# The merge of attention branches: its elementwise work from GpSimd to VectorE, its PSUM banks from the scores' pool

## The chip, the cores and the metric

One core of one Trainium2 chip runs the whole program. The metric is the time of one execution on the device in microseconds; the kernel before has a median of 3433.43 us over three runs (3427.34 to 3434.07).

## The reference, cut to what matters

One step of a hybrid decoder layer over a prompt of 2048 tokens and a sample group of 8 x 8 tokens. Half of the layer's mixing width is dilated sliding-window attention (8 heads of 64), the other half an RWKV-7 recurrence. Then come the output projection and an MLP. In the attention every head evaluates three key sets ("branches" b = 0, 1, 2 with window and dilation (128,1), (512,4), (2048,16)) and merges their outputs by their softmax denominators:

```python
mall = max(maxs[0], maxs[1], maxs[2])
for mx, dn, o in zip(maxs, dens, outs):
    sc = jnp.exp(mx - mall)
    num = num + sc[..., None] * o
    den = den + sc * dn
out = num / den[..., None]
```

## The kernel before

The kernel runs in stages: input projection and recurrence, the attention of the prompt (from about 1218 to 1760 us of the span), the output projection with the sample's attention, the MLP. The change is in the attention of the prompt. The order of the instructions on each engine isn't written out by hand: the Tile framework lays it out ahead of time, by the order of the program as priority and with a planner's own costs for when each operand is there. On the chip each engine then runs its queue in order, and waits on semaphores. A pool's tiles are given out in the order of the program; a tile asked for while all of its pool's buffers are taken waits for a release.

Four calls of `attention(p, ...)` (L1056), one for each pair of heads, each run three branches of four groups; a group is two steps (branches 0 and 1) or one (branch 2), so a call has twenty steps. A step makes score tiles on TensorE (PE) in the PSUM pool "sc" (L1087, L1088, three banks), adds the bias and takes the row minimum on VectorE (DVE, L1090), takes exponentials on ScalarE (ACT), transposes (L1105, pool "pt", two banks), copies back by ACT or DVE in turn, and multiplies with the values into "o" (L1112, two banks). After each group ACT copies o to `ob[b]` (L1116 to L1120). The tile ob[0] has two buffers, ob[1] and ob[2] one each.

`merge(p, ob, st)` (L1127) is a generator; its steps run during the next call, two for each `pump()` (L1390) at the end of an attention step. It spreads row statistics over groups (`zst` L1135, `mv2` L1136, on GpSimd, POOL), brings them into a common layout by small products (L1144, L1149, L1155), copies these to `sw` by ACT, takes minimum, exponentials, denominators and weights on DVE and ACT, sends the weights through DRAM (wD, wrow, L1190 and L1193), and then, for four groups of columns and three branches, spreads them over partitions by a product (L1200), multiplies ob[b] by them on DVE (L1201) and adds up the branches (L1203). The merge of call 3 runs after the attention.

The same `pump()` also advances `recurrent_half()` (L1232) by one step, by two at every eighth: the recurrent rows' part of the output projection. It loads weights and inputs by DMA on SP's queue, splits them in two parts on POOL (L1239, L1240, tiles fm and fw), makes 64 groups of twelve products (L1263) in the PSUM pool "ax", which has one bank, adds the residual on DVE (L1265, tile fr) and stores to rD (L1266). The merges of calls 0 to 2 take their PSUM tiles from "ax" too; that of call 3 takes them from "sc".

After the prompt's attention, `sample_attention` (L1279) loads cached keys and values, with its own PSUM pools "sp" and "ax" in the banks that the attention has left, and the products of the output projection (L1541) run beside it; the last columns of the projection need the sample's result.

Of the kernel before, what the change touches and what calls it, by code (L numbers as in the profile page):

```python
# [9 lines left out]
F32 = mybir.dt.float32  # L10
F32R = mybir.dt.float32r
AF = mybir.ActivationFunctionType
ALU = mybir.AluOpType
# [4 lines left out]
P = 128  # L18
# [12 lines left out]
def bc(ap, axis, n):  # L31
    a = ap.unsqueeze(axis)
    shape = list(a.shape)
    shape[axis] = n
    return a.broadcast_to(shape)
# [136 lines left out]
def _build(ctx, tc, nc, I, O, dbg, upto):  # L172
    V, S, PE, G = nc.vector, nc.scalar, nc.tensor, nc.gpsimd
# [4 lines left out]
    def tsc(out, in0, s1, s2, op0, op1):  # L178
        V.tensor_scalar(out, in0, s1, s2, op0, op1)

    def tt(out, a, b, op):
        V.tensor_tensor(out, a, b, op)  # L182

    def act(out, in_, func, bias=0.0, scale=1.0, **kw):
        S.activation(out, in_, func, bias=bias, scale=scale, **kw)  # L185

    def pool(**kw):
        if kw.get("space") is not DRAM:
            kw["reuse_waits"] = "tile"
        return tc.tile_pool(**kw)  # L190
# [798 lines left out]
    psc = ph2.enter_context(pool(name="psc", bufs=3, space=PSUM, side="right"))  # L989
    ppt = ph2.enter_context(pool(name="ppt", bufs=2, space=PSUM))  # L990
    pax = ph2.enter_context(pool(name="pax", bufs=1, space=PSUM))
# [64 lines left out]
    def attention(p, pump, ahead):  # L1056
# [66 lines left out]
        if p < 3:  # L1123
            ahead["bias", p + 1, 2] = bias_load(p + 1, 2)
        return merge(p, ob, st)

    def merge(p, ob, st):  # L1127


        def mp():  # L1130
            return psc.tile([P, 512], F32, name="sc") if p == 3 else pax.tile([P, 512], F32, name="ax")

        for ty in range(2):
            for x in range(2):
                G.tensor_tensor(zst[:, x, :, :, 4 * ty:4 * ty + 4], bc(st[:, x, 1, :, ty, :].rearrange("p g q -> p q g"), 3, 4), bc(bc(mk1, 1, 4), 1, 4), ALU.mult)  # L1135
                G.tensor_tensor(mv2[:, ty, x], bc(st[:, x, 2, :, ty, :], 3, 8), bc(bc(rr2, 1, 4), 1, 4), ALU.mult)  # L1136
            yield
        sw = at.tile([P, 6, P], F32, name="sw")
        ps = mp()
        flat = st.rearrange("p x b g t c -> p (x b g t c)")  # L1140
        for x in range(2):
            for g in range(4):
                c0 = x * 96 + g * 8
                PE.matmul(ps[32 * g:32 * g + 32, x * P:x * P + P], flat[:, c0:c0 + 32], ident, start=True, stop=True, tile_position=(0, 32 * g))  # L1144
        for x in range(2):
            for q in range(4):
                for g in range(4):
                    c0 = 256 + x * P + q * 32
                    PE.matmul(ps[32 * g:32 * g + 32, c0:c0 + 32], zst[:, x, q, g], rr1, start=True, stop=True, tile_position=(0, 32 * g))  # L1149
        act(sw[:, 0:4].rearrange("p a n -> p (a n)"), ps, AF.Copy)  # L1150
        yield
        ps = mp()
        for g in range(4):
            for ty in range(2):
                PE.matmul(ps[32 * g:32 * g + 32, 0:256], d2[:, g, ty], mv2[:, ty].rearrange("p x g c m -> p (x g c m)"), start=(ty == 0), stop=(ty == 1), tile_position=(0, 32 * g))  # L1155
        act(sw[:, 4:6].rearrange("p a n -> p (a n)"), ps[:, 0:256], AF.Copy)
        yield

        def nat(x, b):
            v = sw[:, 2 * b + x]  # L1160
            return v if b == 0 else v.rearrange("c (q n) -> c n q", q=(0, 4, 16)[b])

        def alike(ap, b):
            return ap if b == 0 else ap.rearrange("c (n q) -> c n q", q=(0, 4, 16)[b])

        nall = at.tile([P, P], F32, name="nall")
        V.tensor_copy(nall, nat(0, 0))
        for b in (1, 2):
            tt(alike(nall, b), alike(nall, b), nat(0, b), ALU.min)
        sc = at.tile([P, 3, P], F32, name="scw")  # L1170
        for b in range(3):
            tt(alike(sc[:, b], b), alike(nall, b), nat(0, b), ALU.subtract)
        act(sc, sc, AF.Exp)
        yield
        dn = at.tile([P, P], F32, name="dn", tag="nall2")
        dm = at.tile([P, P], F32, name="dm", tag="nall")
        tt(dn, sc[:, 0], nat(1, 0), ALU.mult)
        for b in (1, 2):
            tt(alike(dm, b), alike(sc[:, b], b), nat(1, b), ALU.mult)
            tt(dn, dn, dm, ALU.add)  # L1180
        tsc(dn, dn, 1e-30, None, ALU.max, ALU.bypass)
        V.reciprocal(dn, dn)
        yield
        tt(sc, sc, bc(dn, 1, 3), ALU.mult)
        wh = at.tile([P, 2, 3, P], F32R, name="wh2", tag="sw")
        act(wh[:, 0], sc, AF.Copy)
        tt(wh[:, 1], sc, wh[:, 0].bitcast(F32), ALU.subtract)
        wD = dat.tile([6, 4, 8, P], F32, name="wD")
        for g in range(4):
            nc.sync.dma_start(out=wD[:, g].rearrange("a r n -> r a n"), in_=wh[32 * g:32 * g + 8].rearrange("p x b n -> p (x b) n").bitcast(F32))  # L1190
        wr = wrow
        for x in range(2):
            nc.sync.dma_start(out=wr[x * 8:x * 8 + 8].bitcast(F32), in_=wD[3 * x:3 * x + 3].rearrange("b g (t c) n -> (g t) b (c n)", t=2))  # L1193
        yield
        yield
        for g in range(4):
            cs = slice(g * 512, (g + 1) * 512)
            for b in range(3):
                ps = mp()
                PE.matmul(ps, wsel[:, g], wr[:, b], start=True, stop=True)  # L1200
                tt(ob[b][:, cs], ps, ob[b][:, cs], ALU.mult)  # L1201
                if b:
                    (V if p == 3 else G).tensor_tensor(ob[0][:, cs], ob[0][:, cs], ob[b][:, cs], ALU.add)  # L1203
                yield
            nc.sync.dma_start(out=mixA[p, :, cs], in_=ob[0][:, cs])

# [17 lines left out]
    mk1, rr1, rr2 = mcon[:, 0:4], mcon[:, 4:36], mcon[:, 36:44]  # L1224
    d2 = mcon[:, 44:].rearrange("p (g t c) -> p g t c", g=4, t=2)
    zst = at.tile([P, 2, 4, 4, 32], F32, name="zst")
    G.memset(zst, 0.0)
    mv2 = at.tile([P, 2, 2, 4, 4, 8], F32, name="mv2")
# [284 lines left out]
    with pool(name="wo2", bufs=1) as wo2, pool(name="pwo", bufs=4, space=PSUM, side="right") as pwo, pool(name="psa", bufs=1, space=PSUM) as psa, pool(name="pst", bufs=1, space=PSUM) as pst:  # L1513
# [8 lines left out]
        for c0 in range(0, NT, NC_):  # L1522
# [3 lines left out]
            g, q0 = c0 // (2 * HT), c0 % (2 * HT)  # L1526
# [238 lines left out]
```

## Time and profile before

| quantity | value |
|---|---|
| median of three runs | 3433.43 us |
| profiled execution | 3430.08 us |
| its span, first to last instruction | 3428.3 us |
| mean granted clock of TensorE | 0.955 of full speed |
| busy share of PE, DVE, ACT, POOL | 92%, 63%, 43%, 31% |

Times of the trace are microseconds from the start of the span. A PE that counts as busy isn't PE at its peak, since matmuls are pipelined. The rows below come from the views of windows (busy time of each engine in a stretch), of waits (who waited for whom), of the timeline (instructions in order of time) and of the groups by line.

### The profile page before, as it was taken

The page shows a single profiled execution, that of the slowest core. Times are in us where ns is not written, and L with a number is a line of the kernel's source. Part 1 is how long each engine was busy: PE and PEld are TensorE (multiplying, and loading weights), DVE is VectorE, ACT ScalarE, POOL GpSimd, SP SyncE. Part 2 cuts the span into 40 slices and gives each one's busy share as a digit, 9 for nine tenths or more (in the row PEclk, how much of TensorE's full clock was granted, in tenths as well). Part 3 has the DMA queues.
Part 4 walks back from the last instruction along what each step waited for, and adds up shares of the span by engine and source line. Part 5 has one row for each costly group of instructions (what it writes and reads, how often), then busy time and mean ns, then how long its engine had stood idle before and what let it go on. Part 6 is the DMA issues. An engine that isn't in the chain of part 4 may idle for free.

```text
span 3428.3 us, 64759 instructions
## 1 busy us (share of the span) xinstructions
PE 3165.2 (92%) x24406; PEld 2883.9 (84%) x24406; DVE 2171.6 (63%) x4576; ACT 1465.3 (43%) x3468; POOL 1071.6 (31%) x1311
## 2 busy tenths in 40 slices
PE   5999999989988889897989789999999999999999
PEld 5877867887887878686868579999999999899999
DVE  4656686776675444353556666767776666967675
ACT  4555565555454356262532333323333333423232
POOL 1004431343044111323210133333543333534342
PEclk9999999999998999897989889999999999999999
DMA  5465575465455575343457722222232222322122
GB/s 165 136 193 153 132 202 151 115 164 161 129 152 134 162 230 170 93 153 98 113 198 262 288 82 93 87 62 87 70 128 71 75 74 75 105 62 87 62 87 71
DMA packets 374493, 439.73 MB, mean 128 GB/s; under 512 B 120067, under 2 KB 236734, under 8 KB 374180
## 3 DMA queue, kind: packets, MB, share of 16 engines
q1 hardware_dynamic: 374180, 435.59, 42.4%
q8 instruction: 192, 3.15, 0.4%
q14 instruction: 121, 0.99, 0.1%
HBM read 338.07 MB, written 102.11 MB: 128 GB/s over the span
## 4 chain that ended last, share of the span: by engine, by line
PE 71%; DVE 11%; DMA 9%; issue 3%; SPq 3%; POOL 2%; ACT 2%; DVEq 0%; ACTq 0%; POOLq 0%
PE pm L1696 20%; PE pm L1628 17%; PE pj L335 8%; PE pj L803 4%; PE ax L1263 3%; PE o L1112 3%; PE pwo L1541 3%; PE pt L1105 2%; PE sc L1087 2%; PE sc L1088 2%; DVE ml L182 1%; DMA wr<-in_wq 1%; DMA xg<-in_xg 1%; DVE rl L1493 1%; DVE ob L182 1%
## 5 line engine op out<-in xcount | busy, mean ns | idle before, releaser
L185 ACT ACTIVATE wh<-wr 128x512 fp32r<-128x512 f32 x744 | 463.4, 625 | 823.9 <-PE pm L1696 474.3
L1696 PE MATMUL pm<-fh,wl 128*128 128x352 f32 x1536 | 496.4, 323 | 8.6 <-DVE wl L1571 8.6
L1696 PE MATMUL pm<-fh,wh 128*128 128x352 f32 x1536 | 493.6, 324 | 0.0
L1696 PE MATMUL pm<-fl,wh 128*128 128x352 f32 x1536 | 492.7, 323 | 0.4 <-DVE fl L182 0.4
L1628 PE MATMUL pm<-mh,wh 128*128 128x352 f32 x1344 | 437.1, 326 | 13.8 <-ACT wh L185 11.7
L1628 PE MATMUL pm<-mh,wl 128*128 128x352 f32 x1344 | 433.9, 324 | 5.3 <-DVE wl L1571 5.3
L1628 PE MATMUL pm<-ml,wh 128*128 128x352 f32 x1344 | 434.5, 324 | 3.3 <-DVE ml L182 3.3
L182 DVE TENSOR_TENSOR res<-pm,res 128x352 f32<-128x352 f32 x384 | 198.4, 522 | 288.2 <-PE pm L1696 285.5
L1571 DVE TENSOR_TENSOR wl<-wr,wh 128x512 fp32r<-128x512 f32 x432 | 364.3, 843 | 12.9 <-ACT wh L185 10.0
L1696 PEld LDWEIGHTS pm<-fh,wl 128*128 128x128 f32 x1536 | 290.2, 189 | 9.6 <-DVE wl L1571 9.4
L1696 PEld LDWEIGHTS pm<-fl,wh 128*128 128x128 f32 x1536 | 289.3, 189 | 1.2 <-DVE fl L182 1.0
L1696 PEld LDWEIGHTS pm<-fh,wh 128*128 128x128 f32 x1536 | 289.4, 189 | 0.7 <-ACT fh L185 0.2
L1628 PEld LDWEIGHTS pm<-mh,wh 128*128 128x128 f32 x1344 | 254.9, 190 | 14.9 <-ACT wh L185 12.0
L1628 PEld LDWEIGHTS pm<-mh,wl 128*128 128x128 f32 x1344 | 254.4, 189 | 8.5 <-DVE wl L1571 8.4
L1628 PEld LDWEIGHTS pm<-ml,wh 128*128 128x128 f32 x1344 | 255.1, 190 | 5.0 <-DVE ml L182 4.9
L803 PE MATMUL pj<-wh,nh 128*128 128x256 f32 (+1 forms) x816 | 242.2, 298 | 9.6 <-ACT qn L185 7.3
L803 PE MATMUL pj<-wh,nl 128*128 128x256 f32 (+1 forms) x816 | 241.5, 296 | 5.0 <-DVE nl L182 4.8
L1575 POOL TENSOR_TENSOR wr<-wr 128x512 f32<-128x512 f32 x48 | 63.0, 1313 | 578.9 <-DVE wl L1571 470.2
L803 PE MATMUL pj<-wl,nh 128*128 128x256 f32 (+1 forms) x816 | 241.2, 296 | 0.1
L335 PE MATMUL pj<-nh,wh 128*128 128x512 f32 (+3 forms) x600 | 222.0, 373 | 20.3 <-ACT nh L185 10.2
L182 DVE TENSOR_TENSOR wl<-wr,wh 128x512 fp32r<-128x512 f32 (+1 forms) x216 | 149.9, 696 | 134.9 <-ACT wh L185 131.6
L1090 DVE CUSTOM_DVE_ANT_0 e<-sc,bt 128x256 f32<-128x256 f32 (+1 forms) x384 | 133.3, 363 | 147.5 <-PE sc L1088 111.3
(327 smaller groups left out, 7609.2 us busy)
## 6 DMA issues: line engine op xcount, KB each, us to landing
wr<-in_w SPq DMA_DIRECT2D x384, 256.0 KB
wr<-in_wr SPq DMA_DIRECT2D x120, 256.0 KB
wr<-in_wq SPq DMA_DIRECT2D x96, 256.0 KB
kv<-in_kc SPq DMA_DIRECT2D x40, 512.0 KB
kv<-in_vc SPq DMA_DIRECT2D x40, 512.0 KB
xsD<-xst SPq DMA_DIRECT2D x56, 256.0 KB
xrkv<-xsD SPq DMA_DIRECT2D x32, 384.0 KB
vt<-vD SPq DMA_DIRECT2D x48, 256.0 KB
```

The costliest lines, as they stand in the source:

```text
L182: V.tensor_tensor(out, a, b, op)
L185: S.activation(out, in_, func, bias=bias, scale=scale, **kw)
L335: PE.matmul(ps[:m, :n], a[:, k, :m], b[h * 4 + k][:, c0:c0 + n], start=(h == 0 and i == 0), stop=(h == 1 and i == 11))
L803: PE.matmul(out, a[h * 2 + k][:, i * P:i * P + m], b[:, k, :], start=(h == 0 and q == 0 and i % 2 == 0), stop=(h == 3 and q == 5 and (i % ...
L1087: PE.matmul(ps[:, c0:c0 + n], cols(qst, b, i, False), cols(kst, b, i, both), start=True, stop=False)
L1090: V.tensor_tensor_reduce(out=e[:, c0:c0 + n], in0=ps[:, c0:c0 + n], in1=bts[ty][:, bts[ty].shape[1] - n:], scale=-1.0, scalar=3e38, op0=AL ...
L1112: PE.matmul(o[ty * 64:ty * 64 + 64, (i % 4) * P:(i % 4 + 1) * P], kv[:, ty * 64:ty * 64 + 64], ptss[ty][:, y * P:(y + 1) * P], start=fst, ...
L1263: PE.matmul(ps[:, :FT], w[k][a][:, o * P:(o + 1) * P], m[k][b], start=(i == 0), stop=(i == 11))
L1541: PE.matmul(ps[:, :NC_], a[k][:, o * P:(o + 1) * P], b, start=(i == 0), stop=(i == 11))
L1571: (G if pooled else V).tensor_tensor(wl, w, wh.bitcast(F32), ALU.subtract)
L1628: PE.matmul(ps, a[:, k], b[:, k], start=(n == 0), stop=(n == 11))
L1696: PE.matmul(ps, a[:, f], b[:, cs], start=(i == 0), stop=(i == 11))
```

## The change

In `merge`, the PSUM tile comes from the scores' pool "sc" for all four calls, not only for call 3. The spreading of statistics (L1135, L1136) and the adds of branches (L1203, on VectorE for call 3 already) go from GpSimd (G) to VectorE (V). What is computed stays the same.

```diff
         def mp():
-            return psc.tile([P, 512], F32, name="sc") if p == 3 else pax.tile([P, 512], F32, name="ax")
+            return psc.tile([P, 512], F32, name="sc")
 
         for ty in range(2):
             for x in range(2):
-                G.tensor_tensor(zst[:, x, :, :, 4 * ty:4 * ty + 4], bc(st[:, x, 1, :, ty, :].rearrange("p g q -> p q g"), 3, 4), bc(bc(mk1, 1, 4), 1, 4), ALU.mult)
-                G.tensor_tensor(mv2[:, ty, x], bc(st[:, x, 2, :, ty, :], 3, 8), bc(bc(rr2, 1, 4), 1, 4), ALU.mult)
+                V.tensor_tensor(zst[:, x, :, :, 4 * ty:4 * ty + 4], bc(st[:, x, 1, :, ty, :].rearrange("p g q -> p q g"), 3, 4), bc(bc(mk1, 1, 4), 1, 4), ALU.mult)
+                V.tensor_tensor(mv2[:, ty, x], bc(st[:, x, 2, :, ty, :], 3, 8), bc(bc(rr2, 1, 4), 1, 4), ALU.mult)
             yield
...
                 PE.matmul(ps, wsel[:, g], wr[:, b], start=True, stop=True)
                 tt(ob[b][:, cs], ps, ob[b][:, cs], ALU.mult)
                 if b:
-                    (V if p == 3 else G).tensor_tensor(ob[0][:, cs], ob[0][:, cs], ob[b][:, cs], ALU.add)
+                    V.tensor_tensor(ob[0][:, cs], ob[0][:, cs], ob[b][:, cs], ALU.add)
```

## Rows read from the trace of the kernel before

**Rows 1.** Windows of the four attention calls: stretch, length, engines' busy, clock, DMA

```profile
1217.60:1322.80 105.20, 103.79 (x765) 90.30 (x766) 51.51 (x237) 69.42 (x239) 18.46 (x37) 0.98 0.61 199
1322.80:1477.00 154.20, 137.36 (x1021) 117.15 (x1021) 67.51 (x260) 66.38 (x228) 37.64 (x60) 0.89 0.42 132
1477.00:1628.60 151.60, 131.10 (x953) 109.61 (x952) 65.07 (x254) 67.49 (x228) 44.82 (x76) 0.85 0.38 118
1628.60:1760.30 131.70, 124.48 (x1027) 106.43 (x1031) 69.23 (x257) 69.94 (x228) 31.47 (x46) 0.92 0.39 108
```

**Rows 2.** Waits from 1210 to 1800: who waited for whom, us, times, longest

```profile
POOL fmh L1239 <- PE ax L1263: 109.2, 13, 21.1
ACT ob L185 <- POOL ob L1203: 92.7, 3, 40.9
...
POOL mv L1136 <- DVE st L1090: 46.7, 6, 19.0
```

**Rows 3.** Window of one stopped stretch, columns as in group 1

```profile
1399.00:1437.00 38.00, 21.36 (x62) 14.32 (x62) 9.98 (x16) 0.55 (x3) 14.86 (x19) 0.61 0.28 84
```

**Rows 4.** ACT's timeline in call 1: start, length, instruction, idle before and its end

```profile
1382.49 0.60 ACT L185 ACTIVATE sw<-ax 128x512 f32<-128x512 f32 x1
...
1436.85 1.08 ACT L185 ACTIVATE ob<-o 128x512 f32<-128x512 f32 x2 [37.45 <-POOL ob L1203]
```

**Rows 5.** PE's timeline in the same stretch

```profile
1404.66 0.77 PE L1200 MATMUL ax<-wrow,wsel 128*128 128x512 f32 x1 [5.05 <-DMA wrow<-wD]
...
1411.04 0.56 PE L1263 MATMUL ax<-fmh,fwh 128*128 128x264 f32 x1 [0.87 <-DVE ob L182]
```

**Rows 6.** Groups by line, 1210 to 1800: busy us, mean ns, idle before

```profile
L1203 POOL TENSOR_TENSOR ob<-ob,ob 128x512 f32<-128x512 f32 x24 | 30.6, 1274 | 66.8 <-DVE ob L182 66.7
...
L1136 POOL TENSOR_TENSOR mv<-st,mcon 128x128 f32<-128x128 f32 x16 | 7.2, 455 | 47.9 <-DVE st L1090 46.7 <-ACT e L185 0.9
...
L1203 DVE TENSOR_TENSOR ob<-ob,ob 128x512 f32<-128x512 f32 x8 | 5.3, 683 | 0.0
...
L182 DVE TENSOR_TENSOR dm<-scw,sw 128x128 f32<-128x128 f32 x8 | 3.1, 392 | 0.1
```

**Rows 7.** Timeline of call 3's merge: PE's first two, DVE's last

```profile
1753.10 0.64 PE L1144 MATMUL sc<-ident,st 128*32 128x128 f32 x16
...
1777.45 0.93 PE L1200 MATMUL sc<-wrow,wsel 128*128 128x512 f32 x3 [0.23 <-DMA wrow<-wD]
...
1792.90 0.68 DVE L1203 TENSOR_TENSOR ob<-ob,ob 128x512 f32<-128x512 f32 x1
```

**Rows 8.** The half's adds 1, 17, 33, 64 of 64 on DVE; one POOL split

```profile
1281.10 0.43 DVE L182 TENSOR_TENSOR fr<-ax,fr 128x264 f32<-128x264 f32 x1 [1.58 <-issue]
...
1390.64 0.43 DVE L182 TENSOR_TENSOR fr<-ax,fr 128x264 f32<-128x264 f32 x1
...
1405.34 0.74 POOL L1240 TENSOR_TENSOR fml<-fr,fmh 128x264 fp32r<-128x264 f32 x1
...
1529.02 0.43 DVE L182 TENSOR_TENSOR fr<-ax,fr 128x264 f32<-128x264 f32 x1
...
1751.74 0.43 DVE L182 TENSOR_TENSOR fr<-ax,fr 128x264 f32<-128x264 f32 x1 [1.39 <-PE ax L1263]
```

**Rows 9.** PE: the sample's first output products; last projection products (chain that ended last)

```profile
1773.76 1.93 PE L1342 MATMUL ax<-kv,pts 128*32 128x128 f32 x32
...
1951.54 5.93 DMA kv<-in_kc
...
1965.89 2.33 PE ax L1342 x56
1969.82 17.23 PE pwo L1541 x96
```

**Rows 10.** DVE's scw products beside POOL's, and with POOL idle (timeline)

```profile
1389.32 1.22 DVE L182 TENSOR_TENSOR scw<-nall,sw 128x128 f32<-128x128 f32 x3
...
1389.27 1.02 POOL L1135 TENSOR_TENSOR zst<-st,mcon 128x64 f32<-128x64 f32 x3 [0.63 <-DVE st L1090]
...
1759.40 0.89 DVE L182 TENSOR_TENSOR scw<-nall,sw 128x128 f32<-128x128 f32 x3
```

## The prediction

> **What bounds the kernel now.** I read the attention stage call by call first, with the windows of the four calls of attention [rows 1]. The calls have the same twenty steps each, yet they take 105.2, 154.2, 151.6 and 131.7 us. The first one has no merge beside it; the later three run with the merge of the call before. Together they are 122 us longer than three clean calls would be. In them PE's granted clock falls from 0.98 to between 0.85 and 0.92, and ACT's busy time does not grow (69.4 us, then 66 to 70): the surplus is waiting and not work.
>
> The view of the waits tells where [rows 2]: ACT sits 92.7 us before three evacuations of the attention's output into ob, 40.9 us the longest, and what ends each wait is the merge's add of branches on POOL (L1203). ob[1] and ob[2] have one buffer each, so this call's branch 1 can't be written before the merge of the last call has read the old one; ACT runs in order, so all exponentials stand behind that copy. In such a stretch of 38 us DVE is busy 10 us, ACT 0.55, and the granted clock is 0.61 on the mean, between its two levels of 1.2 and 2.4 GHz (0.5 and 1.0), while PE waits for DVE between products [rows 3, 5].
>
> Why is the merge so late? In ACT's timeline the merge of call 0 copies its first sums (sw) at 1382.5, about 60 us after call 0 ended at 1322.8 [rows 1, 4]. Its input had been there all that time. What it lacked is the bank "ax". That pool has one bank, shared with the recurrent half of the output projection (L1263), and is given out in program order: two merge steps, then one step of the half. The half is behind (it begins with weight loads) and 16 of its 64 products stand ahead of the merge. Later the twelve products of L1200 go through the same bank one at a time, with L1263 products among them: the first at 1404.7, an L1263 at 1411.0 that starts only when DVE has emptied the bank [rows 5], the last copy-back released at 1436.9 [rows 4]. So a merge costs one trip PE, DVE, PE per tile, 32 us for twelve, beside a stopped attention.
>
> **The change part by part.** *PSUM bank.* For calls 0 to 2 the merge takes "sc" (three banks) and leaves "ax" to the half. How that behaves is shown by the merge of call 3, which already does so, with its adds on VectorE: first product 1753.1, right at the end of the scores; first L1200 at 1777.5; last add ends at 1793.6 [rows 7]. That is 24 us of chain (sums, minimum, exponential, reciprocal, two trips through DRAM) and 16 us for twelve products with eight adds, 40.5 us in all, where the merge of call 0 needed 1436.9 - 1322.8 = 114 us. In a call, branch 1's first copy into ob comes after ten of twenty steps, half of a 105 us call or less: some 40 to 52 us. So a merge that starts at once ends about when ob[1] is wanted. The stall goes from about 37 us to between 0 and 10.
>
> *Adds on VectorE.* Eight per merge, 24 in the three calls: 1274 ns on POOL, 683 ns on DVE [rows 6]. POOL loses 30.6 us, DVE gains 16.4 us.
>
> *Spreading of weights.* Sixteen L1135 and sixteen L1136 in four merges. The trace has no such form on DVE; the nearest row is dm, a DVE product of 128x128 with a strided operand, 392 ns, and the same instruction takes 455 ns on POOL [rows 6]. I take 0.4 for all of them, 0.2 and 0.46 as the ends: eight per merge, 3.2 us (1.6 to 3.7). They are hidden as long as DVE has room. Something is won beside it: on POOL the mv instructions wait 46.7 us for the attention's last scores [rows 2], and POOL's casts for the half stand behind them. On DVE the same wait would hold scores; but there the instructions that they wait for precede them on the same engine, except the row sums from ACT, a fraction of a microsecond each. I price that at nothing, at most 1 us per instruction, 8 per merge.
>
> *DVE's room.* A clean call has DVE busy 51.5 of 105.2 us; call 1 with its merge 67.5 [rows 1]. After the change it is 67.5 + 8 x 0.68 + 3.2 = 76 us. That is 72% of 105, so DVE does not bound the call, but the merge's work falls into its first half: 24.5 us on top of about 26 in some 50. It nearly fills DVE there and I add 5 to 10 us for it. So a call with a merge becomes about 110 us; the first call's 105.2 holds a start on DMAs that later calls don't have, so the lower end is 100.
>
> *Port.* DVE's three scw products took 1.22 us together while three POOL products ran, and 0.89 us with POOL idle [rows 10], so two-input DVE instructions do lose time to POOL. The Trainium skill, "SBUF — State Buffer", section "SBUF: two separate sides", says that such a DVE operation and a GpSimd operation that reads SBUF exclude each other for the whole instruction. This trace agrees in direction (0.33 us for three). By that rule the 24 added DVE adds would hold POOL's casts up to 24 x 0.68 = 16 us, and if all of it lay on the half's chain the time would be 16 us above my forecast.
>
> *End of the stage.* Calls 1 to 3 at 110 us end at 1322.8 + 330 = 1653 instead of 1760.3: 107 us earlier. Merge 3's first product, 7 us before that end, moves from 1753.1 to 1646.
>
> *What is late next: the half.* After the change the half no longer gains ground while attention stands still. Its 64 DVE adds run from 1281.1 to 1751.7, so now it ends together with attention. The first 16 take until 1390.6: 6.85 us per add; the 33rd, behind the second load of weights, comes at 1529.0 [rows 8]. I leave that one where it is. With 6.85 per add, 17 more are done by 1646; 14 remain. With attention gone they go faster: in the stretch where attention had just stopped, the first add of one column block was at 1390.6 and the operands of the next block were ready at 1406.1 [rows 8]; with one product that is about 17.5 us per four, 4.4 per add. So it ends at 1646 + 14 x 4.4 = 1708; at the old pace it would be 1742. POOL's casts, free of the waiting mv and of the adds, should give some of it back: I take 1700.
>
> *What hangs on it.* The sample's attention needs "ax" banks for its output: its first product there is at 1773.8, 20.7 us after merge 3's first product and 22 us after the half's last add. From there on the sample is a chain in which key loads still stand on the path near its end, until its last product ends and the last 96 products of the output projection follow at 1969.8 [rows 9]; these need the sample's result. So all that follows moves with that 1773.8. After: the later of 1646 + 21 = 1667 and 1700 + 1 = 1701. The sum is 1773.8 - 1701 = 73 us less. The projection, the MLP and their rows are untouched.
>
> The profiled execution took 3430.1 us (span 3428.3 and 1.8 around it), 3.4 below the median of 3433.4. 3430.1 - 73 = 3357, and in terms of the median 3360. With the half's end between 1685 and 1742 this case reaches from 3345 to 3402; most of it lies below 3385.
>
> **Rivals.** *The half keeps up*: the freed bank and POOL let it gain as fast as attention does; attention's end bounds. Sample at 1667, 107 us less: 3326, and 3311 if a call takes 105. For it: 13 casts on POOL wait 109.2 us for "ax" products in the trace [rows 2], and the merges leave that bank. Against it: the weight loads and its single set of operands stay.
>
> *The score banks are held*: L1200's tile is given out in program order, before wrow has come back from DRAM, and scores wait for banks, or PE stands in order before L1200 as it does 5 us at 1404.7 [rows 5]. Price: the 24 us of the chain [rows 7] per merge, so a call takes 105 + 24 = 129, merge 3's first product comes at 1703, the sample at 1724: 50 us less, 3383. With DVE's queue on top, up to 3405. Against it: call 3's merge starts so late only because scores are over, and three banks serve two score tiles per step.
>
> *It doesn't do what it says*: the planner sets the merge as late as before, since something other than the bank holds it. Then only the trips shorten or not even these: 3420 to 3435.
>
> *Slower*: the half bounds and gets slower. Its adds queue on DVE behind 20 merge instructions in a row, its store of rD waits for them in SP's in-order queue, and its next loads stand behind the store. From 1529.0 on it took 7.2 us per add with merges beside it [rows 8]. It decides from 7.9 us per add: (1772.8 - 1529.0)/31. At 8.3 the half ends at 1786 and the sample starts 13 us late: 3446.
>
> **How the numbers follow.** Forecast 0.42; the half keeps up 0.20; banks held 0.20; doesn't do what it says 0.08; slower 0.10. The predicted time is the forecast's, 3360. The range leaves out the last two cases and the tip of the second: 3312 to 3408. Faster by over 0.2% (7 us, about what a measurement of this kernel can tell from no change): the first three and a little of the fourth, 0.83; within: 0.07; slower: 0.10.
>
> **What would show it.** Right: the waits list has ACT's ob copies before L1203 at under 30 us in all; sw copies stand within 10 us of each call's end; the calls' windows are 105 to 115 us at a clock over 0.95; the half's last add comes 40 to 60 us after the last score; the sample's first "ax" product follows it directly. Wrong: idle time of PE before L1200 on wrow or of scores on banks, with calls near 130 (banks held); half and attention ending together near 1650 (it keeps up); sw still 50 us late (no effect); the half's last add past 1773 (slower).

## The result, and the profile after

The changed kernel takes 3387.2 us (median of 4 runs, 3380.1 to 3393.3) beside 3431.9 of the kernel before (4 runs): a ratio of 0.987, 95% interval 0.985 to 0.989, or 45 us less. The profiled execution took 3393.3 us with a span of 3391.6; it is the longest of the four, so its trace shows 37 of these 45 us. The head of its page:

```profile
span 3391.6 us, 64731 instructions
...
PE 3148.3 (93%) x24406; PEld 2877.4 (85%) x24406; DVE 2187.3 (64%) x4632; ACT 1465.1 (43%) x3468; POOL 1034.9 (31%) x1255
```

**The calls.** Windows of the four calls of attention in the kernel after, beside [rows 1] (stretch, length, busy time of PE, PE's loads, DVE, ACT and POOL, granted clock, DMA share and GB/s):

```profile
1222.30:1327.80 105.50, 104.82 (x766) 91.19 (x766) 52.65 (x245) 69.34 (x239) 15.59 (x28) 0.96 0.60 198
1327.80:1458.00 130.20, 126.11 (x1050) 110.99 (x1049) 72.00 (x275) 68.19 (x230) 25.67 (x44) 0.99 0.49 157
1458.00:1587.40 129.40, 121.53 (x926) 105.50 (x926) 70.50 (x272) 66.75 (x227) 34.11 (x60) 0.96 0.45 142
1587.40:1714.40 127.00, 121.80 (x1036) 104.79 (x1034) 72.01 (x269) 68.97 (x228) 18.26 (x30) 0.96 0.41 109
```

The three calls with a merge went from 437.5 us to 386.6, and the clock of call 2 from 0.85 to 0.96. This execution enters the attention 4.7 us later than that of before, so 46 us of the 51 arrive at the end of the stage: the last score product moves from 1752.7 to 1707.1.

**The stall.** The waits of the kernel after from 1210 to 1800, beside [rows 2] (who waited for whom, total us, times, longest):

```profile
POOL fmh L1239 <- PE ax L1263: 153.4, 12, 21.4
ACT e L185 <- DVE st L1090: 134.7, 142, 10.0
...
ACT ob L185 <- PE o L1112: 28.0, 31, 3.0
...
PE sc L1200 <- DMA wrow<-wD: 11.8, 4, 5.8
```

ACT's wait for the merge's adds (L1203), 92.7 us before, is gone: no row of this view has it. Where the merge starts is seen in ACT's timeline of call 1, beside [rows 4]; its first sums are copied at 1333.7, 5.9 us after call 0 ended, where it had been 60:

```profile
1333.73 0.60 ACT L185 ACTIVATE sw<-sc 128x512 f32<-128x512 f32 x1
...
1359.41 0.51 ACT L185 ACTIVATE e<-e,st 128x256 f32<-128x256 f32 x1 [9.12 <-DVE st L1090]
```

The second line is the new loss: ACT stands 9.1 us without scores, in the middle of branch 0. PE's timeline of the same stretch tells why. The score products (L1087, L1088) stop at 1343.6 and go on at 1357.9, right behind the merge's products of weights (L1200), which wait for the weights to come back from DRAM. In between PE works mostly for the half (L1263, about forty products, first and last shown):

```profile
1343.63 0.28 PE L1088 MATMUL sc<-klo,qst 128*128 128x256 f32 x1
1343.75 0.29 PE L1263 MATMUL ax<-fmh,fwh 128*128 128x264 f32 x1
...
1354.44 0.28 PE L1263 MATMUL ax<-fmh,fwh 128*128 128x264 f32 x1
1356.95 1.19 PE L1200 MATMUL sc<-wrow,wsel 128*128 128x512 f32 x2 [2.23 <-DMA wrow<-wD]
1357.94 0.41 PE L1087 MATMUL sc<-kst,qst 128*128 128x256 f32 x1
```

I counted the gaps of more than 5 us between score products, from the start of one L1087 to the start of the next. Before there was one per merge, of 48.5, 53.1 and 25.7 us. After there are two: 8.9, 9.3 and 8.0 us at the merge's sums, and 14.5, 12.7 and 10.3 us at its products of weights.

**The half and the sample.** In the tile "ax" of the kernel after, beside [rows 8, 9] (durations least/median/most, then first and last start), the half's 64th add comes 26 us before the last score product, and the sample's first product 25 us behind it, at 1732.2 instead of 1773.8:

```profile
L1342 PE MATMUL ax<-kv,pts x704: 267/273/423, 1732.2 to 1929.3; 128*32 128x128 f32 x160, 8*32 8x128 f32 x16
...
L182 DVE TENSOR_TENSOR fr<-ax,fr x64: 368/433/434, 1286.1 to 1680.8; 128x264 f32<-128x264 f32 x64
```

### The profile page after: what moved, and what is told of

Same layout as the page of the kernel before. It is cut to its first block, busy times and chain, and to the rows that moved or that the text cites. A ratio compares the mean times of both kernels' runs of the same rounds, so it can differ in the third digit from the quotient of the medians.

```text
span 3391.6 us, 64731 instructions
## 1 busy us (share of the span) xinstructions
PE 3148.3 (93%) x24406; PEld 2877.4 (85%) x24406; DVE 2187.3 (64%) x4632; ACT 1465.1 (43%) x3468; POOL 1034.9 (31%) x1255
## 5 line engine op out<-in xcount | busy, mean ns | idle before, releaser
L1628 PE MATMUL pm<-mh,wh 128*128 128x352 f32 x1344 | 437.5, 326 | 14.4 <-ACT wh L185 12.2
L803 PE MATMUL pj<-wh,nh 128*128 128x256 f32 (+1 forms) x816 | 241.1, 296 | 10.7 <-ACT qn L185 7.4
L185 ACT ACTIVATE e<-e,st 128x256 f32<-128x256 f32 (+1 forms) x384 | 174.9, 456 | 137.0 <-DVE st L1090 134.7
```

What stands on the lines that cost most here:

```text
L803: PE.matmul(out, a[h * 2 + k][:, i * P:i * P + m], b[:, k, :], start=(h == 0 and q == 0 and i % 2 == 0), stop=(h == 3 and q == 5 and (i % ...
L1628: PE.matmul(ps, a[:, k], b[:, k], start=(n == 0), stop=(n == 11))
```

## The experiments

All are against the kernel before, measured beside it: 3426.5 us beside e1 to e4, 3431.3 beside e5 to e8, 3432.7 beside e9 to e11, 3429.4 beside e12. So rows of different groups are compared by their ratios, and a few microseconds between their medians say nothing. "Empty steps" are steps of the merge's generator in which it does nothing, so that what follows is given out later in the program.

| run | edit | median us | ratio, 95% interval |
|---|---|---|---|
| after | the change | 3387.2 | 0.987 (0.985 to 0.989) |
| e1_bank_only | bank alone | 3379.4 | 0.986 (0.985 to 0.988) |
| e2_engines_only | engines alone | 3432.0 | 1.001 (1.000 to 1.003) |
| e4_ax_products | after, products of weights in "ax" | 3407.7 | 0.994 (0.993 to 0.996) |
| e5_early2 | after, products two steps earlier | 3389.7 | 0.988 (0.986 to 0.990) |
| e9_late2 | after, two empty steps ahead of the products | 3377.6 | 0.984 (0.983 to 0.986) |
| e3_late4 | four | 3365.4 | 0.983 (0.981 to 0.985) |
| e10_late8 | eight | 3352.7 | 0.977 (0.976 to 0.979) |
| e12_late14 | fourteen | 3366.8 | 0.981 (0.979 to 0.983) |
| e6_late4_pool | bank alone, four | 3365.4 | 0.981 (0.979 to 0.983) |
| e8_late4_sw2 | e3, and two ahead of the sums | 3362.5 | 0.980 (0.978 to 0.982) |
| e11_late4_sw2_pool | e6, and two ahead of the sums | 3369.0 | 0.982 (0.980 to 0.983) |
| e7_light_half | e3, the half without its work | 3295.0 | 0.960 (0.958 to 0.963) |

**Which part of the change does it?** The two parts alone.

```diff
--- e1: the kernel before, with
-            return psc.tile([P, 512], F32, name="sc") if p == 3 else pax.tile([P, 512], F32, name="ax")
+            return psc.tile([P, 512], F32, name="sc")
--- e2: the kernel before, with V for G in zst, mv2 and the adds, the bank as it was
```

> The bank's part of the change alone: merges take their PSUM tiles from the scores' pool, adds and spreading stay on GpSimd. Theory A (the scores' banks are given to the products of L1200 while their weights are still on the way through DRAM, so scores pause 10 to 14 us per call): the pause stays, calls 1 to 3 take 125 to 132 us, the time is 3380 to 3395, as with the whole change. Theory B (VectorE is overfull in branch 0): VectorE has some 9 us less per call, calls take 115 to 121, the time is about 3360.

> The engines' part alone: adds and spreading on VectorE, merges of calls 0 to 2 still in the half's single bank. If the single bank is what made merges late, the statistics are still copied 40 to 60 us after a call's end, ACT still waits about 30 us or more per merge before ob, and the time is 3420 to 3435. If GpSimd (its in-order queue or its slower adds) was what made them late, the waits shrink to under 15 us per merge and the time is below 3400.

The bank alone gives all of the gain, the engines alone none. e1 came near theory A: its time is 0.6 us under that range, and two of its calls (118 and 135 us) lie outside 125 to 132. In e2's waits the stall stands as before, with DVE's name in place of POOL's:

```profile
ACT ob L185 <- DVE ob L1203: 89.0, 3, 39.1
```

In e1 it is gone, though POOL keeps the spreading (zst, mv2) and is held by it as before:

```profile
POOL zst L1135 <- DVE st L1090: 41.8, 8, 16.2
...
POOL mv L1136 <- DVE st L1090: 28.0, 6, 13.2
```

e1 also has the pauses of the scores (14.5, 11.4 and 15.8 us at the products), so these too come with the bank.

**What holds the scores?** Theory A: the products' tiles are given out in program order, so they hold score banks from then until the weights are back. Theory B: DVE is too full beside the merge. Three kernels: the products given out four steps later; only the products in "ax" again; the products two steps earlier.

```diff
--- e3: the kernel after, with
         yield
         yield
+        for _ in range(4 if p < 3 else 0):
+            yield
         for g in range(4):
--- e4: the kernel after, with
-                ps = mp()
+                ps = mp() if p == 3 else pax.tile([P, 512], F32, name="ax")
--- e5: the kernel after, with
-        yield
-        yield
+        if p == 3:
+            yield
+            yield
         for g in range(4):
```

> The changed kernel with four more empty steps (two attention steps, about 10 us) ahead of the products of L1200 in the merges of calls 0 to 2, so that their banks are asked for when the weights are back. Theory A: the pause of the scores falls from 10 to 14 us to under 4, calls take 115 to 122, the time is 3350 to 3362, or about 3370 if the recurrent half now ends last. Theory B: the same VectorE work lies in the same branch, calls stay at 127 to 131, the time at 3380 to 3392. If the delay pushes the merge's end past the first copy into ob[1], ACT waits on L1203 again, by up to 10 us per call.

> The changed kernel with the products of L1200 in calls 0 to 2 back in the half's single bank, the merge's statistics still in the scores' pool. Theory A: scores don't pause, since no bank of theirs is held, but the twelve products go one at a time with the half's products among them as before, some 25 to 33 us, from about 30 us after the call's start: ACT waits 5 to 20 us per call before ob[1]; the time is 3380 to 3410. If the lateness of the statistics alone had been the harm of the single bank, the time would be 3360 or less.

> The changed kernel without the two empty steps that stand between the weights' DMA and the products of L1200 in the merges of calls 0 to 2: the products ask for their banks one attention step (about 5 us) earlier, the weights come back when they did. Theory A (banks of the scores held during the weights' trip): the second pause of the scores grows from 10 to 14 us to 14 to 20, the time by 8 to 18 us against the changed kernel's 3387, to 3395 to 3405. Theory B (VectorE overfull): the same work in the same branch, 3381 to 3393.

In e3 no wait of PE for the weights is left, and the gaps at the products shrink to 4.8, 6.6 and under 4.5 us (under 4 was forecast); those at the sums stay at 7 to 9. The time falls by 22 us between the medians (by 15 between the ratios), to between the 3362 and the 3370 that theory A had named; the calls (122, 117 and 126 us) are a little longer than its 115 to 122. e4 frees the scores and gets the old loss back: its first product of weights is multiplied at 1395.5, and ACT waits for the adds again, 27 us the longest where 5 to 20 per call was forecast:

```profile
ACT ob L185 <- DVE ob L1203: 53.4, 3, 27.0
```

What binds the scores to the products is seen in the order in which PE's queue was laid out. In the rows of the kernel after, further up, no score product stands between 1343.63 and the two products of weights at 1356.95, and the next one stands right behind them. In e4, with the products in "ax", scores stand directly ahead of the product and behind it:

```profile
1394.84 0.40 PE L1088 MATMUL sc<-klo,qst 128*128 128x128 f32 x1
1395.06 0.43 PE L1200 MATMUL ax<-wrow,wsel 128*128 128x512 f32 x1
1395.33 0.29 PE L1087 MATMUL sc<-kst,qst 128*128 128x128 f32 x1
```

That it is the three banks that set this order is concluded from the program and from e4: the rows don't show which bank a product writes.

e5 missed its forecast in the time: 3389.7 us is the changed kernel's within the noise. In its first merge the pause began 3.3 us earlier but the weights were back 3.8 us earlier too, so it stayed as long; in the other two it grew (14.1, 13.9 and 15.0 us, where the changed kernel has 14.5, 12.7 and 10.3). Calls 1 to 3 took 395.0 us in its trace instead of 386.6, about the 8 us at the lower end of theory A's forecast; what follows the attention was 10 us shorter in that execution and hid it.

**The same delay, in more sizes, and with the other engines.** e9, e10 and e12 are e3 with 2, 8 and 14 for the 4; e6 is e1 with e3's edit.

> The changed kernel with two empty steps (one attention step) ahead of the products of L1200 in the merges of calls 0 to 2, half of the late variant's delay. Theory A (score banks held during the weights' trip; the second pause of the scores, 10 to 14 us with no delay and gone with four steps, depends on when the products ask): a pause of 4 to 9 us, the time about halfway, 3370 to 3382. Theory B (VectorE overfull): no dependence, but the late variant has already spoken against it.

> The changed kernel with eight empty steps (four attention steps): no banks held, but the merge ends at the fourteenth step, four after the first copy into ob[1]. If that wait is what bounds from the other side, ACT waits 5 to 20 us per call on L1203, and the time goes up again against four steps' 3365, to 3370 to 3390. If the two banks of o and the planner's order cover it, 3360 to 3368.

> The changed kernel with fourteen empty steps ahead of the products instead of none, for calls 0 to 2 (eight gave 3352.7 us, four 3365.4, two 3377.6, none 3387.2). Theory A, the delay wins by not holding score banks while the weights are in DRAM, and there is nothing left to win once the weights are back when the first tile is given out; from there on the products only come later and ACT's first copy of branch 1 into ob waits for the merge's last add again: the waits list shows ACT's ob copies before the adds again, some 5 to 20 us in each of three calls, and the time is 3360 to 3395 us. Theory B, the delay wins because the merge's work on VectorE is spread and falls into a quieter part of the call: no such wait, and the time falls on to 3340 to 3350 us.

> Merges in the scores' pool with the four empty steps, but adds and spreading on GpSimd as before: only the engine differs from the late variant at 3365. If VectorE's room costs what the prediction said (5 to 10 us per merge, of which the moved work is a third to a half), branch 0 gets 2 to 5 us shorter and the time is 3350 to 3362. If the engine makes no difference, 3360 to 3370. If GpSimd's in-order queue delays the recurrent half, the half ends after the attention and the time is 3368 to 3380.

With 0, 2, 4, 8 and 14 steps the time is 3387, 3378, 3365, 3353 and 3367 us. Two steps leave gaps of 10.7, 11.8 and 6.2 us at the products (4 to 9 was forecast), eight none over 4.5 us. The whole time also holds what varies elsewhere: ahead of the attention all kernels are the same, and yet it begins between 1210.5 and 1222.3 us in the traces. The calls themselves, between ACT's last copies of o into ob, show the effect more plainly. These are sums over calls 1 to 3 in us, one execution each:

| steps more | run | calls | of it branch 0 | branch 1 |
|---|---|---|---|---|
| 2 fewer | e5 | 395.0 | 170.1 | 140.8 |
| 0 | after | 386.6 | 158.4 | 141.8 |
| 2 | e9 | 381.8 | 149.9 | 144.7 |
| 4 | e3 | 364.9 | 129.5 | 139.5 |
| 8 | e10 | 358.9 | 125.6 | 139.7 |
| 14 | e12 | 365.7 | 125.3 | 151.3 |

The products stand in branch 0, and it gets shorter with every step of delay until the weights are back in time. Theory B can't explain that: in e3 the first multiplication of each merge on DVE starts 31 to 32 us behind the end of the last call, in the changed kernel 30 us, so DVE gets the same work at nearly the same time, and branch 0 is still 29 us shorter, 10 per call. So A holds. Neither of e10's two forecasts covers its time, 13 us below e3's; 6 of these lie in the calls, and e3 still had the two gaps of 4.8 and 6.6 us. In e10 scores and products alternate on PE:

```profile
1354.43 0.37 PE L1087 MATMUL sc<-kst,qst 128*128 128x128 f32 x1
...
1356.35 0.48 PE L1202 MATMUL sc<-wrow,wsel 128*128 128x512 f32 x1
1356.66 0.28 PE L1087 MATMUL sc<-kst,qst 128*128 128x128 f32 x1
...
1358.01 0.48 PE L1202 MATMUL sc<-wrow,wsel 128*128 128x512 f32 x1
```

The second half of e12's theory A holds in the time, not in the sign that I named. ACT waits for the adds for 0.6 us in all; but the copies of branch 1 into ob that need these adds were laid out later in ACT's queue, two at once. The same line of ACT's timeline in e10 and then in e12:

```profile
1389.24 1.06 ACT L185 ACTIVATE ob<-o 128x512 f32<-128x512 f32 x2
```

```profile
1407.60 1.09 ACT L185 ACTIVATE ob<-o 128x512 f32<-128x512 f32 x2
```

Branch 1 is longer for it, by 12 us in the three calls, and the calls as a whole by 7, since branch 2 gets shorter. (Of the 15 us between the two profiled executions, 5 arise ahead of the attention, where nothing was changed.) So there is a best point: late enough that the weights are back, early enough that ob[1] is free. e10 is the fastest version run, 34 us below the changed kernel.

e6 answers for the engines again: 3365.4 us with adds and spreading on POOL, 3365.4 with both on DVE. But the equal times hide a trade. With both on POOL the three calls take 355.3 us instead of 364.9 (branch 0 128.5 instead of 129.5, so not there), and the half's last add comes at 1697.2, 28 us behind the last score product, instead of 1680.5. The condition of e6's third forecast, a half that ends after the attention, came true; its time did not. The other pairs show the same: in e1 beside the changed kernel, and in e11 beside e8, the calls are 7 to 10 us shorter with POOL and the half ends 15 to 25 us later.

**The pause at the sums.** Two empty steps ahead of the first sums, on e3 and on e6.

```diff
--- e8: e3, and e11: e6, each with
             yield
+        for _ in range(2 if p < 3 else 0):
+            yield
         sw = at.tile([P, 6, P], F32, name="sw")
```

> The late variant with two more empty steps (one attention step) ahead of the first statistics product, so that its two banks are asked for after the last exponentials of the call before. If banks held for statistics make the first pause (7 to 9 us at each call's start), it shrinks to under 5 us and the time falls by 5 to 12 us, to 3353 to 3360. If the pause is only PE's queue, it moves with the products and stays, 3362 to 3370. If the merge now ends after branch 1's first copy, ACT waits on L1203, and the time is 3368 to 3380.

> Four empty steps ahead of the products, two ahead of the statistics, adds and spreading on GpSimd: the two details that each looked like nothing or a few us. If both are real and add up, 3350 to 3358; if neither is, 3360 to 3368.

Neither can be told from its partner (3362.5 beside 3365.4, 3369.0 beside 3365.4; the intervals overlap); e11 lies 1 us above its forecast. The gaps of 7 to 9 us at the sums shrink by 1 to 2 us in two merges, and in the third they grow to 10.8 and 10.9. What this pause costs stays open.

**What does the half cost beside attention?** e3, with the loads, splits, products and adds of the half left out; only its steps and the copies of the residual remain, so the recurrent rows' part of the projection is missing from this kernel's output.

> The late variant with the recurrent half's loads of weights and inputs, their splits, its 768 products and its 64 adds left out (it only copies the residual from input to rD); this part of the result is missing. If the half sets the end of the stage in the late variant (its last add and the last score were both at 1680), the stage ends 15 to 30 us earlier, calls 2 and 3 are as long as they were, and the time is 3335 to 3350. If it only takes room beside attention, the calls get shorter, to 100 to 110 us, and the time is 3315 to 3340. If it does neither, 3358 to 3368.

It came out 20 us below the lower end of that forecast: the half costs more beside attention than I thought. From e3, of which it is the edit, calls 1 to 3 fall from 364.9 to 297.6 us: 67.3 us for 56 groups, 1.2 us each. Its calls 1 to 3, and then those of e10 (columns as above):

```profile
1316.60:1418.80 102.20, 96.58 (x753) 79.99 (x753) 63.29 (x258) 66.30 (x232) 0.00 (x0) 0.93 0.70 226
1418.80:1517.00 98.20, 96.94 (x751) 80.05 (x751) 62.70 (x256) 66.68 (x229) 4.28 (x10) 0.93 0.33 105
1517.00:1614.20 97.20, 94.18 (x765) 77.34 (x765) 62.96 (x246) 66.39 (x221) 0.00 (x0) 0.96 0.26 71
```

```profile
1320.10:1440.10 120.00, 119.61 (x990) 106.28 (x989) 70.93 (x273) 67.20 (x229) 23.42 (x39) 1.00 0.52 161
1440.10:1552.00 111.90, 111.29 (x959) 96.52 (x959) 68.90 (x265) 66.45 (x229) 30.76 (x56) 1.00 0.50 157
1552.00:1679.00 127.00, 126.56 (x1056) 109.86 (x1058) 78.35 (x282) 70.24 (x230) 23.10 (x40) 1.00 0.48 132
```

The length of e10's calls follows the number of the half's groups that fall into them. Its adds in the groups by line, call 0 first and then calls 1 to 3:

```profile
L182 DVE TENSOR_TENSOR fr<-ax,fr 128x264 f32<-128x264 f32 x8 | 3.5, 433 | 10.6 <-issue 8.5 <-PE ax L1265 2.0
...
L182 DVE TENSOR_TENSOR fr<-ax,fr 128x264 f32<-128x264 f32 x20 | 8.6, 431 | 11.0 <-issue 6.3 <-PE ax L1265 4.3 <-PE sc L1088 0.3
...
L182 DVE TENSOR_TENSOR fr<-ax,fr 128x264 f32<-128x264 f32 x13 | 5.6, 431 | 11.9 <-issue 8.8 <-PE ax L1265 3.1
...
L182 DVE TENSOR_TENSOR fr<-ax,fr 128x264 f32<-128x264 f32 x22 | 9.5, 432 | 20.1 <-issue 8.3 <-PE ax L1265 7.8 <-DMA sbias<-svD 3.7
```

20, 13 and 22 groups go with 120.0, 111.9 and 127.0 us; e7 has none and takes 102.2, 98.2 and 97.2. That is 61.3 us for 55 groups, 1.1 us each. The price does not hold for call 0: e7's takes 106.1 us without the half (granted clock 0.90), e10's 105.3 with 8 groups in it (0.96). In the later calls PE is busy for all but 0.4 to 0.6 us in e10, at a granted clock of 1.00, so there PE is what the attention waits for, as far as busy time tells: the ends of products are modelled, and the same attention shows more PE time where it has PE to itself (e7: 94 to 97 us, at a granted clock of 0.93 to 0.96) than PE has left beside the half in e10's call 1 (119.6 - 40.1 = 79.6), where the window of the half's products alone reads (PE, PE's loads, clock, DMA):

```profile
1320.10:1440.10 120.00, 40.05 (x240) 32.90 (x240) 1.00 0.52 161
```

How those 1.1 to 1.2 us come about isn't settled by these runs.

## Why the prediction was right or wrong, point by point

The time, 3387.2, lies in the range (3312 to 3408), and the sign is right. The likeliest case gave 3360; what happened is the rival of the held score banks, priced at 3383, which had 0.20. Of the signs for "right", ACT's wait and the early sums came; the calls of 105 to 115 us did not (127 to 130), nor the half's last add 40 to 60 us after the last score (26 us before it). PE's waits on wrow and calls near 130 are the signs of the held banks.

**The diagnosis held.** It was the single "ax" bank that made the merge late and through it ob[1] that stopped ACT: e1 removes both with the bank alone, e2 keeps both with the engines moved, and the change has ACT's wait at none (under 30 us was the sign) and the first sums 6 to 7 us behind each call's end (within 10).

**The cost of the moved instructions held.** The groups by line of the kernel after, 1210 to 1800, beside [rows 6]:

```profile
L1203 DVE TENSOR_TENSOR ob<-ob,ob 128x512 f32<-128x512 f32 x32 | 22.8, 713 | 0.1
...
L1136 DVE TENSOR_TENSOR mv<-st,mcon 128x128 f32<-128x128 f32 x16 | 4.4, 288 | 0.1
...
L1135 DVE TENSOR_TENSOR zst<-st,mcon 128x64 f32<-128x64 f32 x16 | 3.3, 221 | 0.5 <-ACT e L185 0.4
```

The spreading costs (4.4 + 3.3)/4 = 1.9 us per merge, inside 1.6 to 3.7, and 0.6 us of waiting in all; an add takes 713 ns instead of 683. The port's price, up to 16 us on the half's chain, did not come true: with the adds on DVE the half ended 17 us earlier (e3) than with them on POOL (e6), e6 and e3 take the same time, and e2 stays within 0.3% of before, where 16 us would be 0.5%. POOL's splits (L1240, 128x264) took 803 ns on the mean in the kernel after, from 1322 to 1680, and 764 before: some 2 us in all. The Trainium skill, "SBUF — State Buffer", section "SBUF: two separate sides", has such DVE and GpSimd instructions exclude each other. No run here shows a time of the whole kernel that hangs on it; single instructions do lose time. In the kernel before, the three scw products took 1.85 us together from 1657.6, while POOL's casts and splits ran, against the 0.89 of [rows 10].

**The step that failed: "a call with a merge becomes about 110 us".** The calls took 130, 129 and 127. One term was put at nothing, and one had the wrong cause.
- *The half in the call.* I took the clean call's 105.2 us as what attention needs, and gave the half's work in the later calls no time. e7 and e3 differ in that work alone: 297.6 and 364.9 us for the three calls, 22 us per call. The clean call could not show it: it holds 8 groups where the later ones of the kernel after hold 22, 18 and 16, and e7's call 0, which holds none, is as long (106.1 us). "The surplus is waiting and not work" I read off ACT; PE, busy 103.8 us in the clean call, is busy 124 to 137 in the later three of [rows 1], in part because of the lower clock there (0.85 to 0.92). My working asked whether DVE has room and never asked PE.
- *The held banks.* I put stall and crowding of DVE at 5 to 10 us per call. What goes when the products come late enough is 386.6 - 364.9 = 21.7 us for three calls in e3 and 27.7 in e10, 7 to 9 per call; gaps of 10 to 14 us between scores show where. The size is near mine, the cause isn't: DVE has the same load in e3 as in the changed kernel, and less in e6, whose branch 0 takes as long as e3's. Of e10's 27.7 us, 16 are idle time of PE (17.2 us in the changed kernel's three calls, 1.4 in e10's, by the windows above); for the rest PE was busy longer, at a granted clock of 0.96 to 0.99 against 1.00.

Per call that is 99 us (e7: attention and merge without the half), 22 for the half and 7 for the held banks: 129, as measured on the mean. These are three kernels one edit apart, so the sum has to come out; it says what each part costs and is no test. The rival's price of 129 per call was right by luck: its mechanism carries 7 to 9 us of the 24 that I gave it (the scores stop for 10 to 14 us at the products, not for the whole chain), and it left out the half's 22 us, while the 105 that it starts from lies 6 us above e7's 99.

**The step "the half ends at 1700 and bounds" failed.** The half's adds ran at 5.9 us each for the first 16 and 5.8 from the 33rd to the last, where before it had been 6.85 and 7.2; I kept it at 6.85 beside attention. It ended at 1680.8, and attention, at 1707.1, bounded. With "ax" to itself the half gained. The pauses of the scores at the products don't explain it: in e10, which has none, the adds from the 33rd on also take 5.8 us. In e3 the two end together (1680.5 and 1680.9), in e10 the half 7 us later (1679.2 and 1672.0): there my mechanism may begin to bind, at 1679 and not at 1700. In e6, with the adds on POOL, the half does end last, at 1697.2.

**The step "all that follows moves with the sample's first product" held for the changed kernel, but not in general.** It starts 25.1 us after the last score (before: 21.1; e10: 19.0). It came 41.6 us earlier in the changed kernel and 82.8 in e10; the profiled executions are 36.8 and 78.8 us shorter. In e6 it starts at 1714.9, 15 us later than in e3, and yet the sample's last product ends at 1899.8 in e6 and 1900.3 in e3, and the two take the same time.

**What stays open:** the pause of 8 to 9 us at the merge's sums, how the half's 1.1 to 1.2 us per group reach the attention, why they don't in call 0, and why the calls are shorter with the adds on POOL.

## What to carry to other kernels

A background job that shares a small rotating pool with the main loop takes its place in the pool where the program asks for the tile and not where its operand arrives: ask for the bank only after the data are due back, and sweep that point, since too late has a price as well. When two parts of a change come together, run each alone: here one line carried everything. And before a clean stretch is taken as the price of a stretch with background work, run both stretches once without that work, and look at the busiest engine first, even if it isn't the one that the change loads.

## What the runs showed of the hardware

Two-input products of 128x128 with broadcast operands took 288 ns on DVE and 455 ns on POOL, those of 128x64 221 ns on DVE; I had taken 392 ns from a strided neighbour. And PE's busy share hides such a pause: of the 14.1 us from 1343.8 to 1357.9 in the changed kernel PE is busy 10.7, 6.0 of it for the half, at a granted clock of 0.95, while no score product starts.
